# A hybrid short-convolution and gated linear-attention layer in streamed blocks: how keys and values are turned to token rows

## The chip, the cores and the metric

The kernel runs on one core of a Trainium2 chip. The metric is the device time of one execution in microseconds (us); lower is better. Before the change three executions took 2580.45, 2583.85 and 2586.18 us. The profile that is read below is of a further execution, which took 2583.43 us.

The engines are named as the profile names them: PE is the matrix engine (PEld its weight loads), DVE is VectorE, ACT is ScalarE, POOL is GpSimd, SP is the engine whose queue issues most loads. A trailing q (SPq, POOLq) is the engine's instruction queue.

## What is computed

One layer, float32, over 2048 prompt tokens and 64 sample tokens, width 1024. A wide input projection gives ten parts; four of them feed a three-tap convolution path (path A), four feed a gated linear attention with eight heads of width 128 (path B), two are gates. Both paths are projected, gated, summed and projected again; a normalised, gated residual with a small per-layer embedding follows. What matters here is path B, per head and chunk of 64 tokens:

```python
def hgrn2_block(S, q, k, v, logf):
    b = jnp.cumsum(logf, axis=1)
    ref = b[:, (L - 1) // 2][:, None]
    qe = q * jnp.exp(b - ref)
    ke = k * jnp.exp(ref - b)
    att = jnp.where(causal, jnp.einsum('bthk,bshk->bhts', qe, ke), 0.0)
    o = jnp.einsum('bhts,bshv->bthv', att, v) + jnp.einsum('bthk,bhkv->bthv', q * jnp.exp(b), S)
    S_new = jnp.exp(b_last)[..., None] * S + jnp.einsum('bshk,bshv->bhkv', k * jnp.exp(b_last[:, None] - b), v)
    return S_new, o
```

The last product sums over tokens s. A matmul of PE sums over the 128 partitions, so for it both k and v must lie with tokens on the partitions. The projection leaves them the other way round, with features on the partitions and tokens along the row.

## The kernel before

The 2112 tokens are worked off in three blocks of 768, 704 and 640 (`SIZES`, line 30). Within a block the order is: path B for the eight heads (`path_b`), with the gate projections (`gates`) run between heads as fill; path A (`path_a`); the output projections; the norms. Large projections run by a seven-product scheme: `sgroup` does two columns of weights in seven products of 12 matmuls, and after each product it calls `hook()`, which takes the next small step from a list. The attention of a head is cut into such steps (`head_attn`, a generator with a `yield` after each), and `path_b` writes out by hand which step runs after which product. `placed()` ties a step's matmuls behind the last matmul of the projection, so PE's order is the written one. On the other engines the framework orders the instructions by their dependencies and their place in the program; `tc.issue_after` and `behind_all` add an order on one engine.

`head_prep` makes what a head needs. It runs a projection group for f and v (`sgroup` with `sink_f`), takes the logarithm (line 959), the running sum (line 962), runs the next group for q and the output gate, and in its middle (`scaled`, called at the third product) makes the scaled keys `ka` and `kb`. `queries` then makes `qe` (line 1011 in the first block, 1015 and 1016 in the others) and `qx`, which is `qe` times the chunk factors `f` (line 1017). Chunks go in pairs of 128 tokens: six pairs in the first block, five in each of the others, which the parts of the block take as four and the rest. The middle block also has the 64 sample tokens, which make a part of their own (`single`).

Keys and values come to token rows in two ways.

- In the first block (`first`), and for the sample part: PE transposes each pair of `kb` and of `vt` (lines 1091 and 1093) into PSUM, and ACT copies both out (lines 1095 and 1096).
- In the other two blocks: `turned` lets DVE turn 32 x 32 squares (line 1051) into a scratch tile (`qx` for the values, `b` for the keys, which are free at that time), and POOL's queue writes the result to DRAM (line 1053). `in_rows` reads it back through POOL's queue with the squares moved to their places (line 1058). The values come back with each pair in four runs of 32 elements. The keys come back interleaved: the elements of one pair lie `npair` = 5 elements apart, and `kt[:, i]` takes every fifth. Both reads stand behind both writes and behind the last `pow` on POOL (`behind_all([*wrote, *powers])`).

Then, per part, `head_attn` makes the scores (lines 1106 and 1107), masks them, multiplies keys by values (line 1121, with `kt` as the weights and `v` as the moving operand), updates the states on DVE (line 1138), makes the outputs (line 1161 with `v` moving, line 1163 with `qx` as weights), norms them (POOL has the `pow` in `rstd_of`, line 689), transposes back (line 1179) and multiplies by the gate (line 1181).

Tiles `r` come from one pool of 48 (`RING`), whatever they hold.

Of the kernel before, what the change touches and what calls it, by code (L numbers as in the profile page):

```python
# [14 lines left out]
ALU = mybir.AluOpType  # L15
# [3 lines left out]
P = 128  # L19
# [4 lines left out]
CH = 64  # L24
# [69 lines left out]
def hybrid_step(  # L94
# [17 lines left out]
    V, A, G, T, SP = nc.vector, nc.scalar, nc.gpsimd, nc.tensor, nc.sync  # L112
# [13 lines left out]
    def nm(s):  # L126
        uid[0] += 1
        return f"{s}_{uid[0]}"
# [12 lines left out]
    def sized(bl, steps):  # L141

        while True:
            with sized_to(bl):
                try:
                    made = next(steps)
                except StopIteration:
                    return
            yield made

    def hn():
        return width[0] // 2

    def rt(n=0, dt=F32):
        t = ring.tile([P, BN + 2], dt, tag="r", name=nm("r"))
        return t if n is None else t[:, : n or width[0]]

    def hf(n=0):
        return ring.tile([P, HN], F32, tag="hf", name=nm("hf"), bufs=HALVES)[:, : n or hn()]

    def ps_attn():
        return psa.tile([P, 512], F32, tag="pa", name=nm("pa"))
# [14 lines left out]
    ident = const.tile([P, P], F32, tag="ident", name="ident")  # L177
# [116 lines left out]
    last, hooks, copies, adds, ahead, evicted, freed, powers, means = [None], [], [None], [None], [], [], [], [], []  # L294

    def placed():

        return tc.issue_after(last[0]) if last[0] is not None else nullcontext()
# [7 lines left out]
    def behind_all(marks):  # L306

        order = ExitStack()
        for ins in marks:
            order.enter_context(tc.issue_after(ins))  # L310
        return order
# [383 lines left out]
    def spread(cols, n):  # L695

        pb = ps_attn()
        with placed():
            for i, o in tiles_of(n):
                T.transpose(pb[:, o : o + P], cols[:, i : i + 1].to_broadcast([P, P]), ident)  # L700
        return pb[:, :n]
# [38 lines left out]
    def row_rstd(bl, out):  # L740

        todo = tiles_of(bl["n"])
        full = bl["n"] // P
        cols = small.tile([P, 2, 6], F32, tag="rows", name=nm("rows"), bufs=1)[:, 0, : len(todo)]
        nxt = []
        for n in range(0, len(todo) + 2, 2):
            now, nxt = nxt, []
            for i, o in todo[n : n + 2]:
                xts = [rt(512), rt(512)]
                for q, xt in enumerate(xts):  # L750
                    G.dma_start(xt, x_tok[bl["t0"] + o : bl["t0"] + o + P, q * 512 : q * 512 + 512])
                nxt.append((i, xts))
            for i, xts in now:
                sc = small.tile([P, 2], F32, tag="ss2", name=nm("ss2"), bufs=2)
                with behind_all(copies):
                    for q, xt in enumerate(xts):
                        A.activation(xt, xt, AF.Square, accum_out=sc[:, q : q + 1])
                V.tensor_tensor(sc[:, 0:1], sc[:, 0:1], sc[:, 1:2], ALU.add)
                rstd_of(sc[:, 0:1], cols[:, i : i + 1], 1.0 / D)
            yield  # L760
        pt, t = ps_attn(), rt(P)
        with placed():
            T.transpose(pt[: len(todo), :P], cols, ident)
        A.copy(t[: len(todo)], pt[: len(todo), :P])
        row = dram.tile([BN], F32, tag="xrs", name=nm("xrs"), bufs=2)[: bl["n"]]
        G.dma_start(row[: full * P].rearrange("(i p) -> i p", p=P), t[:full])
        if full < len(todo):
            G.dma_start(row[full * P :].unsqueeze(0), t[full : full + 1, (full + 1) * P - bl["n"] :])
        out.append(row)
        yield  # L770
# [162 lines left out]
    def chunks(t):  # L933
        return t.rearrange("p (c t) -> p c t", t=CH)

    def head_prep(bl, hc, hd, first, hs):
        n, npair = bl["n"], bl["npair"]
        nch, np1 = n // CH, npair * P
        sf, vt = rt(), rt()
# [15 lines left out]
        else:  # L955
            sgroup(FF * 8 + hd, IV * 8 + hd, hc, sink_f, first)
        lg, b, eq, qx = rt(), rt(), rt(), rt()
        wrote = None if first else [turned("tv", vt, qx, npair)]
        A.activation(lg, sf, AF.Ln, bias=lb[:, hd : hd + 1], scale=omlb[:, hd : hd + 1])
        if not first:  # L960
            V.tensor_scalar(sf, sf, nomlb[:, hd : hd + 1], omlb[:, hd : hd + 1], ALU.mult, ALU.add)
# [4 lines left out]
        f, r = qc[:, 0, :nch], qc[:, 1, :nch]  # L966
        ka, kb, qe, z = hf(npair * CH), rt(), rt(), rt()

        def scaled(after):
# [31 lines left out]
            if not first:  # L1001
                wrote.append(turned("tk", kb, b, npair))
# [5 lines left out]
        def queries():  # L1008
            if first:
                A.activation(qe, qe, AF.Silu)  # L1010
                V.scalar_tensor_tensor(qe, qe, QK_SCALE, eq, ALU.mult, ALU.mult)
            else:
                sq = rt()
                A.activation(sq, qe, AF.Sigmoid)
                V.scalar_tensor_tensor(qe, qe, QK_SCALE, sq, ALU.mult, ALU.mult)
                V.tensor_tensor(qe, qe, eq, ALU.mult)
            V.tensor_tensor(chunks(qx), chunks(qe), f.unsqueeze(2).to_broadcast([P, nch, CH]), ALU.mult)

        def sink_q(c, h, x, y):
            if c == 1:  # L1020
# [9 lines left out]
            sgroup(ZB * 8 + hd, QQ * 8 + hd, hc, sink_q, first, mid=scaled, free=first)  # L1030
        with tc.issue_after(freed[0]) if first else nullcontext():
            queries()
        by_token = None
        if not first:
            with behind_all([*wrote, *powers]):
                by_token = [in_rows(kind, npair) for kind in ("tv", "tk")][::-1]
        return dict(
            eq=eq, f=f, ka=ka, kb=kb, qe=qe, qx=qx, vt=vt, z=z, by_token=by_token,
            more=npair - 2 * SWAP, first=first, last=bl["last"], carry=None,
# [2 lines left out]
    def cols3(t, nt):  # L1042
        return t[:, : nt * P].rearrange("p (g c) -> p g c", c=P)
# [3 lines left out]
    def turned(kind, src, out, npair):  # L1047

        n = npair * P
        blocks4 = out[:, :n].rearrange("p (j a g) -> p g j a" if kind == "tk" else "p (j g a) -> p g j a", j=4, a=32)  # L1050
        V.transpose(blocks4, src[:, :n].rearrange("p (g b j) -> p g j b", b=32, j=4))
        turning[kind] = dram.tile([P, n], F32, tag=f"{kind}{npair}", name=nm(kind), bufs=2)
        return G.dma_start(turning[kind], out[:, :n]).ins

    def in_rows(kind, npair):

        t = rt(npair * P)
        G.dma_start(t.rearrange("q (i c) -> q i c", i=4), turning[kind].rearrange("(i b) (j c) -> (b j) i c", i=4, j=4))
        return t.rearrange("q (k g) -> q g k", g=npair) if kind == "tk" else t.rearrange("q (i g a) -> q g i a", i=4, a=32)

    def head_attn(ip, gs, d, hd):

# [2 lines left out]
        nt, ln = len(gs), gs[0]["len"]  # L1065
        o0, n = gs[0]["off"], nt * ln
        qe, z, att = d["qe"], d["z"], atts[ip]
        single = ln < P
        assert (nt == 2 * SWAP) == (o0 == 0)
        rows = slice(P - ln, P)  # L1070

        def tile3(i=None):
            if single and i is not None:
                return lone[i]
            if nt == 1:
                return small.tile([P, 1, P], F32, tag="one", name=nm("one"), bufs=5)
            return cols3(rt(nt * P), nt)

        def cols(t, g):
            end = g["off"] + ln  # L1080
            return t[:, end - P : end]

        if d["by_token"] is not None and not single:
            kt, v = (t[:, o0 // P : o0 // P + nt] for t in d["by_token"])
        else:
            p_k, p_v = ps_attn(), ps_attn()
            with placed():
                for i, g in enumerate(gs):  # L1090
                    T.transpose(p_k[:, i * P : i * P + P], cols(d["kb"], g), ident)
                for i, g in enumerate(gs):
                    T.transpose(p_v[:, i * P : i * P + P], cols(d["vt"], g), ident)
            kt, v = tile3(0), tile3(1)
            A.copy(kt[rows], cols3(p_k, nt)[rows])
            A.copy(v[rows], cols3(p_v, nt)[rows])
        p_a = ps_attn()
        with placed():
            for i, g in enumerate(gs):
# [371 lines left out]
    with tc.high_priority():  # L1471
# [3 lines left out]
        rows, xs, w1 = [], [], {}  # L1475
# [58 lines left out]
    for n in range(4):  # L1534
# [5 lines left out]
        with behind_all(done):  # L1540
            for i in range(3 * n, 3 * n + 3):
                t, total = rows[i], ss[:, i % 2, i // 2 : i // 2 + 1]
# [20 lines left out]
    with behind_all(done):  # L1563
        rs = rt()
        cols = [spread(ss[:, 0, 3 * h : 3 * h + 3], hn()) for h in range(2)]
# [30 lines left out]
    for bi, bl in enumerate(blocks):  # L1596
        first, kept = bi == 0, kepts[bi]
# [7 lines left out]
        a = []  # L1605
        nxt = None if bl["last"] else blocks[bi + 1]
        cols, a_first = [], []
        rows = sized(nxt, row_rstd(nxt, cols)) if nxt else iter(())
# [133 lines left out]
```

## Time and profile before

| what | value |
|---|---|
| median of three executions | 2583.85 us |
| the profiled execution | 2583.43 us |
| its span, first to last instruction | 2581.7 us |
| DVE busy | 1770.1 us, 69% of the span |
| ACT busy | 1491.8 us, 58% |
| POOL busy | 407.0 us, 16% |

How to read it: the span is the part of an execution in which the core's instructions run; the 1.7 us beside it lie around it. Busy times are unions of an engine's instructions. Matmuls overlap in the profile (the next one starts before the end that is shown for the last), so a matmul's price on PE is the distance between the starts of successive matmuls and not the duration that a row gives. In rows of a timeline the columns are start, length, engine, line, operation, tiles (out<-in), shapes and count; in rows of one line they are the shortest, median and longest duration in ns, and the first and last start in us.

### The profile page before, as it was taken

How to read it: one execution, taken by the hardware profiler on the slowest of the kernel's cores; microseconds unless marked ns; L12 is line 12 of the kernel's file. 1: busy time of each engine (PE TensorE's matmuls, PEld its weight loads, DVE VectorE, ACT ScalarE, POOL GpSimd, SP SyncE). 2: the span in 40 equal slices, each digit the busy share in tenths (PEclk: the TensorE clock that was granted, in tenths of full speed). 3: DMA queues.
4: the chain of work that ended last, by engine and by line, in shares of the span. 5: the costliest groups of instructions: out<-in, count | busy, mean ns of one | idle time of the engine just before them, and what ended most of it. 6: DMA issues, size and time to landing. Idle time of an engine off the chain costs nothing.

```text
span 2581.7 us, 47221 instructions
## 1 busy us (share of the span) xinstructions
PE 2562.9 (99%) x16198; PEld 2548.5 (99%) x16198; DVE 1770.1 (69%) x3541; ACT 1491.8 (58%) x2896; POOL 407.0 (16%) x741
## 2 busy tenths in 40 slices
PE   9999999999999999999999999999999999999999
PEld 9999999999999999999999999999999999999998
DVE  7788788898867775476564556887346655336967
ACT  6666666554454763465554555567456665446675
POOL 2011111230022021122111221102111111001011
PEclk9999999999999999999999999999999999999999
DMA  8678777998797887978878998989888898999986
GB/s 328 226 263 303 257 269 264 329 370 295 256 340 255 274 315 264 308 261 272 302 261 288 343 395 312 323 284 338 298 299 285 289 311 277 300 299 320 339 273 201
DMA packets 366865, 760.83 MB, mean 295 GB/s; under 512 B 45142, under 2 KB 49808, under 8 KB 366624
## 3 DMA queue, kind: packets, MB, share of 16 engines
q1 hardware_dynamic: 321696, 582.69, 66.2%
q0 software_dynamic: 44928, 175.12, 18.9%
q8 instruction: 128, 2.10, 0.3%
q14 instruction: 113, 0.93, 0.1%
HBM read 553.92 MB, written 203.71 MB: 293 GB/s over the span
## 4 chain that ended last, share of the span: by engine, by line
PE 90%; issue 3%; DVE 3%; DMA 2%; ACT 1%; POOL 0%; SPq 0%; DVEq 0%; POOLq 0%; ACTq 0%
PE pg L442 19%; PE pg L444 19%; PE pg L443 19%; PE pg L594 4%; PE pg L593 4%; PE pg L595 4%; PE pg L633 3%; PE pg L632 3%; PE pg L631 3%; PE pa L1121 2%; PE pa L1161 1%; PE pa L1163 1%; PE pa L1107 1%; DMA raw<-w_blk 1%; PE pa L1106 1%
## 5 line engine op out<-in xcount | busy, mean ns | idle before, releaser
L442 PE MATMUL pg<-r,hi 128*128 128x320 f32 (+2 forms) x3304 | 1084.3, 328 | 0.0
L443 PE MATMUL pg<-r,hi 128*128 128x320 f32 (+2 forms) x3304 | 1067.9, 323 | 0.0
L444 PE MATMUL pg<-r,lo 128*128 128x384 f32 (+2 forms) x2356 | 768.4, 326 | 2.3 <-DMA lo<-low 2.3
L273 ACT CAST hi<-raw 128x512 fp32r<-128x512 f32 x730 | 449.9, 619 | 507.7 <-PE pg L443 188.1
L442 PEld LDWEIGHTS pg<-r,hi 128*128 128x128 f32 x3304 | 622.9, 189 | 0.9 <-issue 0.2
L443 PEld LDWEIGHTS pg<-r,hi 128*128 128x128 f32 x3304 | 622.3, 188 | 0.0
L444 PEld LDWEIGHTS pg<-r,lo 128*128 128x128 f32 x2356 | 442.9, 188 | 3.2 <-DMA lo<-low 3.2
L444 PE MATMUL pg<-r,s 128*128 128x352 f32 (+1 forms) x948 | 300.6, 317 | 1.7 <-DMA s<-low 1.7
L594 PE MATMUL pg<-r,hi 128*128 128x320 f32 (+2 forms) x864 | 277.4, 322 | 1.9 <-DVE r L226 1.9
L593 PE MATMUL pg<-r,hi 128*128 128x320 f32 (+2 forms) x864 | 274.9, 322 | 0.0
L226 ACT CAST hi<-raw 128x512 fp32r<-128x512 f32 x252 | 155.4, 621 | 167.4 <-PE pg L443 45.6
L226 DVE TENSOR_TENSOR r<-r,r 128x320 fp32r<-128x320 f32 (+7 forms) x354 | 208.9, 609 | 48.7 <-ACT r L226 47.5
L226 ACT CAST r<-r 128x320 fp32r<-128x320 f32 (+7 forms) x354 | 185.5, 557 | 42.7 <-DVE r L1293 8.2
L226 DVE TENSOR_TENSOR lo<-raw,hi 128x512 fp32r<-128x512 f32 x231 | 157.8, 687 | 76.1 <-ACT hi L226 72.5
L444 PEld LDWEIGHTS pg<-r,s 128*128 128x128 f32 x948 | 178.5, 188 | 2.5 <-DMA s<-low 2.4
L595 PE MATMUL pg<-r,lo 128*128 128x352 f32 (+2 forms) x564 | 180.8, 321 | 0.0
L226 ACT CAST hi<-s 128x512 fp32r<-128x512 f32 x156 | 96.6, 619 | 145.4 <-PE pg L443 121.4
L632 PE MATMUL pg<-r,hi 128*128 128x384 f32 (+2 forms) x512 | 167.2, 327 | 0.2 <-DVE r L226 0.2
L594 PEld LDWEIGHTS pg<-r,hi 128*128 128x128 f32 x864 | 162.2, 188 | 4.0 <-DVE r L226 3.6
L631 PE MATMUL pg<-r,hi 128*128 128x384 f32 (+2 forms) x512 | 165.8, 327 | 0.2 <-ACT hi L273 0.2
L456 ACT COPY hf<-pg 128x352 f32<-128x352 f32 (+2 forms) x354 | 157.2, 446 | 11.7 <-PE pg L444 10.7
L593 PEld LDWEIGHTS pg<-r,hi 128*128 128x128 f32 x864 | 161.3, 188 | 1.2 <-ACT r L226 0.6
(398 smaller groups left out, 4120.2 us busy)
## 6 DMA issues: line engine op xcount, KB each, us to landing
raw<-w_blk SPq DMA_DIRECT2D x577, 256.0 KB, 4.4
raw<-S SPq DMA_DIRECT2D x444, 256.0 KB, 4.5
lo<-low SPq DMA_DIRECT2D x422, 256.0 KB, 4.3
s<-low SPq DMA_DIRECT2D x308, 256.0 KB, 4.4
low<-lo SPq DMA_DIRECT2D x271, 256.0 KB, 3.8
S<-s SPq DMA_DIRECT2D x152, 256.0 KB, 3.6
low<-r POOLq DMA_DIRECT2D x54, 256.0 KB, 5.3
r<-w_blk POOLq DMA_DIRECT2D x52, 256.0 KB, 6.5
```

The lines of the kernel that those rows point to most:

```text
L226: return A.copy(hi, src).ins, V.tensor_tensor(lo, src, hi.bitcast(F32), ALU.subtract).ins
L273: A.copy(hi, raw)
L442: add(hi[:, k, :], xhi, start=start and k == 0, stop=False)
L443: add(hi[:, k, :], xlo, start=False, stop=False)
L444: last[0] = add(lo[:, k, :], xhi, start=False, stop=k == KH - 1).ins
L456: copied = A.copy(got[n], ps[bank])
L593: add(hi[:, k, :], xhi, start=start and k == 0, stop=False)
L594: add(hi[:, k, :], xlo, start=False, stop=False)
L595: last[0] = add(lo[:, k, :], xhi, start=False, stop=k == KH - 1).ins
L631: T.matmul(ps, hi[:, k % 4, :], xhi[:, c], start=k == ks[0], stop=False)
L632: T.matmul(ps, hi[:, k % 4, :], xlo[:, c], start=False, stop=False)
L633: last[0] = T.matmul(ps, lo[:, k % 4, :], xhi[:, c], start=False, stop=k == ks[-1]).ins
```

## The change

Four edits, all in path B.

1. `turned` writes the keys' squares in the order that the values have. `in_rows` reads them back in that order, and POOL then copies them into a further tile so that each pair lies in 128 elements side by side. `kt[:, i]` so becomes a row of adjacent elements.
2. In the first block the values, too, are turned by DVE and go through DRAM; its keys are still transposed by PE and copied by ACT.
3. In the first block `qx` is made by POOL, not by DVE.
4. `head_attn` takes from PE what did not come by DRAM: nothing in the later blocks' pairs, the keys in the first block, both for the sample part. Transposes and copies of one operand now stand together.

```diff
-        wrote = None if first else [turned("tv", vt, qx, npair)]
+        wrote = [turned("tv", vt, qx, npair)]
...
-            V.tensor_tensor(chunks(qx), chunks(qe), f.unsqueeze(2).to_broadcast([P, nch, CH]), ALU.mult)
+            (G if first else V).tensor_tensor(chunks(qx), chunks(qe), f.unsqueeze(2).to_broadcast([P, nch, CH]), ALU.mult)
...
-        by_token = None
-        if not first:
-            with behind_all([*wrote, *powers]):
-                by_token = [in_rows(kind, npair) for kind in ("tv", "tk")][::-1]
+        with behind_all([*wrote, *powers]):
+            by_token = [in_rows(kind, npair) for kind in (("tv",) if first else ("tv", "tk"))][::-1]
...
-        blocks4 = out[:, :n].rearrange("p (j a g) -> p g j a" if kind == "tk" else "p (j g a) -> p g j a", j=4, a=32)
+        blocks4 = out[:, :n].rearrange("p (j g a) -> p g j a", j=4, a=32)
...
-        return t.rearrange("q (k g) -> q g k", g=npair) if kind == "tk" else t.rearrange("q (i g a) -> q g i a", i=4, a=32)
+        t = t.rearrange("q (i g a) -> q g i a", i=4, a=32)
+        if kind == "tv":
+            return t
+        kt = rt(npair * P)
+        G.tensor_copy(kt.rearrange("q (g i a) -> q g i a", i=4, a=32), t)
+        return cols3(kt, npair)
...
-        if d["by_token"] is not None and not single:
-            kt, v = (t[:, o0 // P : o0 // P + nt] for t in d["by_token"])
-        else:
-            p_k, p_v = ps_attn(), ps_attn()
+        ready = [] if single else [t[:, o0 // P : o0 // P + nt] for t in d["by_token"]]
+        for q, src in enumerate((d["kb"], d["vt"])[: 2 - len(ready)]):
+            turn_ = ps_attn()
             with placed():
                 for i, g in enumerate(gs):
-                    T.transpose(p_k[:, i * P : i * P + P], cols(d["kb"], g), ident)
-                for i, g in enumerate(gs):
-                    T.transpose(p_v[:, i * P : i * P + P], cols(d["vt"], g), ident)
-            kt, v = tile3(0), tile3(1)
-            A.copy(kt[rows], cols3(p_k, nt)[rows])
-            A.copy(v[rows], cols3(p_v, nt)[rows])
+                    T.transpose(turn_[:, i * P : i * P + P], cols(src, g), ident)
+            ready.insert(q, tile3(q))
+            A.copy(ready[q][rows], cols3(turn_, nt)[rows])
+        kt, v = ready
```

## The prediction, made before the changed kernel ran

> **What bounds the kernel.** The first page gives the engines' shares and the chain of work that ended last.
>
> ```profile
> span 2581.7 us, 47221 instructions
> PE 2562.9 (99%) x16198; PEld 2548.5 (99%) x16198; DVE 1770.1 (69%) x3541; ACT 1491.8 (58%) x2896; POOL 407.0 (16%) x741
> PE 90%; issue 3%; DVE 3%; DMA 2%; ACT 1%; POOL 0%; SPq 0%; DVEq 0%; POOLq 0%; ACTq 0%
> ```
>
> Busy shares alone would not prove that PE is the bound, since matmuls overlap. So the waits come next, those of PE alone, longest total first (total us, times, longest).
>
> ```profile
> PE pa L700 <- POOL cols L689: 3.4, 6, 0.8
> PE pg L444 <- DMA lo<-low: 2.3, 1, 2.3
> ```
>
> The two largest totals are 3.4 and 2.3 us in 2582: PE is fed nearly all the time. A matmul pass that goes away, or is issued closer to the one before, shortens the kernel by as much, unless PE then waits for something new. All the other engines matter only as suppliers.
>
> **The key-value product.** Its line is read for each block by itself, in the order of the blocks.
>
> ```profile
> L1121 PEld LDWEIGHTS pa<-r,r x96: 187/192/192, 103.4 to 471.6; 128*128 128x128 f32 x96
> ...
> L1121 PEld LDWEIGHTS pa<-r,r x80: 297/316/319, 1097.0 to 1360.8; 128*128 128x128 f32 x80
> ...
> L1121 PEld LDWEIGHTS pa<-r,r x80: 302/314/321, 1926.7 to 2161.2; 128*128 128x128 f32 x80
> ```
>
> The same 128x128 weight load takes 192 ns in the first block, where the keys lie side by side, and some 315 ns in the other two, where they lie five elements apart. (There are two passes for each pair: 8 heads x 6 pairs x 2 = 96, and 8 x 5 x 2 = 80.) What this costs PE is read from starts in the timeline, one part of four pairs in the first block and one whole head in the second.
>
> ```profile
> 103.38 0.34 PE L444 MATMUL pg<-r,lo 128*128 128x384 f32 x1
> 103.56 1.05 PE L1121 MATMUL pa<-r,r 128*128 128x128 f32 x8
> 104.36 0.42 PE L442 MATMUL pg<-r,hi 128*128 128x384 f32 x1
> ...
> 1096.95 0.33 PE L444 MATMUL pg<-r,lo 128*128 128x352 f32 x1
> 1097.12 2.33 PE L1121 MATMUL pa<-r,r 128*128 128x128 f32 x10
> 1099.20 0.41 PE L442 MATMUL pg<-r,hi 128*128 128x352 f32 x1
> ```
>
> From the projection's matmul before to the one after: 0.98 us for eight side-by-side passes, 2.25 us for ten interleaved ones. Two more side-by-side passes would cost 0.22 us at the 0.11 us of a transpose (next fence), so ten would take 1.20 us. **Saved: 1.05 us a head, 16 heads, 16.8 us.**
>
> **The values' transposes in the first block.**
>
> ```profile
> 95.80 0.60 PE L1091 MATMUL pa<-ident,r 128*128 128x128 f32 x4
> 96.23 0.60 PE L1093 MATMUL pa<-ident,r 128*128 128x128 f32 x4
> 96.67 0.39 PE L1106 MATMUL pa<-r,hf 128*128 128x128 f32 x2
> ...
> L1093 PE MATMUL pa<-ident,r x48: 272/272/273, 96.2 to 463.2; 128*128 128x128 f32 x48
> ```
>
> Four value transposes hold PE for 0.44 us, 0.11 each. All 48 of the first block go: **5.3 us saved.** The 16 copies by ACT that go with them are off the path, and their going is counted as nothing. Together 22.1 us.
>
> **The key copy on POOL.** This is the one new link on a short chain: the DRAM read lands, POOL copies 128x640, PE loads the weights. Before, PE read the landed tile directly. Here are the reads of the keys that open the second and the third block and that of the third block's last head, each with its time to landing, then the product of that last head; the third block's first product starts at 1926.7 by the third row of the second fence above, the second block's at 1097.0.
>
> ```profile
> 1085.90 0.76 POOL L1058 DMA_DIRECT2D r<-tk  x1 [3.67 <-DMA tk<-r]
> ...
> DMA to landing us min/median/max: 6.9/6.9/6.9
> ...
> 1918.61 0.76 POOL L1058 DMA_DIRECT2D r<-tk  x1 [4.23 <-PE pg L444]
> ...
> DMA to landing us min/median/max: 6.7/6.7/6.7
> ...
> 2151.69 0.76 POOL L1058 DMA_DIRECT2D r<-tk  x1 [4.17 <-issue]
> 2152.44 0.19 POOL L889 COPY r<-hist_p 128x2 f32<-128x2 f32 x1
> ...
> DMA to landing us min/median/max: 6.8/6.8/6.8
> ...
> 2159.36 2.35 PE L1121 MATMUL pa<-r,r 128*128 128x128 f32 x10
> ```
>
> The slack, from landing to weight load, is 1097.0 - 1092.8 = 4.2 us in the second block's first head; worked out in the same way for each head, that block never has less than 4.0. In the third block it is 1926.7 - 1925.3 = 1.4 in the first head and, the load being 0.15 before the product at 2159.36, 2159.2 - 2158.5 = 0.7 in the last; the six between are 2.3, 2.5, 1.0, 2.6, 13.9 and 2.8. What must fit into it is the copy and POOL's reaction to a landing. For the reaction there is a row: the keys' write before the last read, and its landing.
>
> ```profile
> 2144.99 0.60 POOL L1053 DMA_DIRECT2D tk<-r  x1 [6.08 <-DVE r L1051]
> ...
> DMA to landing us min/median/max: 6.2/6.2/6.2
> ```
>
> It landed at 2151.2, and the read that waited for it began at 2151.69: 0.5 us. DVE gives back about 0.1: the turns of line 1051 (row below) go from 1.32 to 1.46 us, the values' at the short end and the keys' at the long one, and the keys get the values' form. So 0.4 plus the copy.
>
> The copy itself is nowhere in this trace. The nearest rows on POOL:
>
> ```profile
> 62.26 0.20 POOL L202 MEMSET r<- 128x128 f32 x1
> 62.53 0.48 POOL L203 TENSOR_SCALAR_AFFINE_SELECT r<-r 128x128 f32<-128x128 f32 x1
> ...
> 60.63 1.69 POOL L203 TENSOR_SCALAR_AFFINE_SELECT r<-r 128x128 f32<-128x128 f32 x2
> ...
> L916 POOL COPY hist_p<-r 128x2 f32<-128x2 f32 x24 | 6.5, 269 | 343.6 <-DVE r L896 343.6
> ```
>
> A copy of two elements takes 0.27 us and a fill of 128 takes 0.20, so the fixed part is some 0.2 us. A select over 128 elements, which reads and writes like a copy and computes besides, takes 0.48 us in one case and 1.69 for the two others, 0.85 each: 2.2 to 5 ns an element above the fixed part. Carried to 640 elements: 1.6 to 3.2 us. From below, the fill may be all fixed part, and then the copy is hardly over 0.3. A copy is the simplest of these, so I take the faster select: **1.6 us**. Then 2.0 us must fit. PE waits 0.6 + 1.0 + 1.3 = **2.9 us** in three heads of the third block, nothing in the second. At 0.3 us nothing waits; at 3.2 us (3.6 to fit) it is 2.2 + 1.3 + 1.1 + 2.6 + 1.0 + 0.8 + 2.9 = 11.9 us.
>
> [...]
>
> Behind the waiting copy on POOL: in the last head the short copy of line 889 (start 2152.44, above) would stand up to 8 us later if it is queued behind; its reader on ACT comes a projection group later. One such place in each of two blocks, taken as nothing; without that cover it costs a microsecond.
>
> **The first block's new work.** DVE gets a turn and loses a product in each head.
>
> ```profile
> 60.00:460.00 400.00, 400.00 (x2476) 399.00 (x2475) 327.84 (x648) 262.83 (x510) 53.36 (x92) 1.00 0.76 266
> ...
> L1051 DVE STREAM_TRANSPOSE r<-r x32: 1319/1380/1464, 1066.6 to 2143.3; 128x640 f32<-128x640 f32 x32
> ...
> L1017 DVE TENSOR_TENSOR r<-r,qc 128x768 f32<-128x768 f32 x8 | 7.6, 951 | 0.0
> ...
> 112.78 1.76 DVE L962 TENSOR_TENSOR_SCAN r<-keep,r 128x768 f32<-128x768 f32 x1 [1.41 <-ACT r L959]
> ```
>
> In 400 us of the first block DVE (the third engine, 327.84 us) is busy 82%. The turn of 768 elements is 1.32 x 768/640 = 1.6 us, against 0.95 that goes: +0.65 us a head, 5.2 in all. The turn falls just ahead of the running sum, where DVE idles 1.41 us for ACT's logarithm; what is not covered there costs DVE some 0.2 us, and PE nothing, as DVE is idle for a sixth of the stretch. Without this cover a late weight split would cost PE up to 1.6 us a head, 12.8 us.
>
> The values must be back before line 1121, and `qx` before line 1163. The second head, whose sum is the row above:
>
> ```profile
> 134.82 0.95 DVE L1017 TENSOR_TENSOR r<-r,qc 128x768 f32<-128x768 f32 x1
> ...
> 155.72 1.05 PE L1121 MATMUL pa<-r,r 128*128 128x128 f32 x8
> ...
> 163.79 0.39 PE L1163 MATMUL pa<-r,r 128*128 128x128 f32 x2
> ```
>
> The values are turned by about 113. A write and a read of some 7 us each end near 127, 28 us before 155.72. Even a read that POOL issues only behind its own product, at about 137, would land by 145. `qx` has 29 us; were POOL four times as slow as DVE, 4 us, it would be hidden. Only the first head is short: its product by keys is at 103.56, its `qx` at about 96.5, so a read behind that product would cost it once some 4 us. Value: nothing. The 16 transfers of 384 KB add 6 MB to 761; PE's waits for DMA, above, are so few that I count nothing.
>
> **Sum**, against the profiled execution's 2583.4 us: - 16.8 - 5.3 + 2.9 = 2564.2 us. The median of the runs is 0.4 above that execution, so 2564.5. With the copy's bounds the sum runs from 2561.7 to 2573.6.
>
> **The rivals.**
>
> *The copy is slow.* At the slower select's rate PE waits 11.9 us: 2573.6. For it speak two of three selects; against it, that a copy computes nothing. 13 in 100.
>
> *The copy eats the gain (slower).* Place: the wait of line 1121 in the third block, then in the second as well. With seven heads whose slack sums to 13.3 us the loss is 7 x (copy + 0.4) - 13.3, and beyond 4.0 us to fit the second block adds its own. It equals 22.1 us at a copy of 4.4 us; from there the kernel is slower. At 6 us the third block loses 31.5 and the second 10.1: 2603. For it: POOL's instructions are uneven (0.48 and 0.85 us for one select). Against: it takes twice the slower select's rate. 9 in 100. [...]
>
> *DVE is too full in the first block.* Each turn delays a weight split: up to 12.8 us lost, 2577. Against it stands the idle sixth. 7 in 100.
>
> *The spacing of the keys isn't what slows line 1121.* The values' four runs of 32 differ between the blocks, too. Then only the 5.3 us are saved, less up to 2.9 for the copy: 2578.5 to 2581.4, no change. Against it: it is the weight load, of keys, that grew from 192 to 315 ns. 5 in 100.
>
> **How the numbers follow.** The forecast has 66 in 100. About 0.2%, 5 us, is what a measurement of this kernel can tell from no change, so faster means below 2578.7: the forecast, the slow copy and most of the full DVE, 84 in 100. Within 0.2%: the spacing and the rest of DVE, 7. Slower: 9. The range runs from 2557 (the sum with a copy that is wholly hidden, less the runs' own scatter of some 4) to 2576 (the slow copy, with 2.5 on top).
>
> **What would show it.** Right: line 1121's weight loads at 190 ns in all blocks, ten passes in 1.2 us; line 1093 without the first block's 48; PE's waits with a new entry, line 1121 for POOL, of about 3 us, all in the third block; POOL copies of 128x640 of about 1.6 us. Wrong: a copy over 3 us, PE waiting for it in the second block, PE waiting for DVE's weight splits between 60 and 460 us, or weight loads still at 300 ns.

## The result, and the profile after

| | before | after |
|---|---|---|
| median of six executions each, in turn on one chip | 2582.76 us | 2561.78 us |
| lowest to highest | 2580.45 to 2586.18 | 2558.75 to 2564.96 |
| the profiled execution | 2583.43 | 2561.54 |

After against before is 0.9918, with a 95% interval of 0.9905 to 0.993: 21.0 us, or 0.8%, faster. The forecast was 2564.5 us.

The head of the page of the changed kernel:

```profile
span 2559.8 us, 47168 instructions
...
PE 2540.1 (99%) x16150; PEld 2525.1 (99%) x16150; DVE 1778.2 (69%) x3541; ACT 1485.7 (58%) x2880; POOL 451.0 (18%) x781
```

PE has 48 matmuls fewer and 22.8 us less to do, ACT 16 instructions fewer. POOL has 44 us more. PE stays the bound: it is busy for 99% of the span, and the largest totals of its waits are 4.1 and 3.2 us. These waits (total us, times, longest), the longest two and those of line 1106:

```profile
PE pg L444 <- DMA lo<-low: 4.1, 3, 2.3
PE pa L700 <- POOL cols L689: 3.2, 6, 0.8
...
PE pa L1106 <- ACT r L1095: 1.0, 1, 1.0
PE pa L1106 <- DVE r L1016: 0.8, 1, 0.8
```

The entry that the prediction looked for, line 1121 waiting for POOL, is not in the list at all. One small entry is new: line 1106 once waits 1.0 us for ACT's copy of line 1095. Next, the product's weight loads block by block (shortest, median and longest ns, first and last start) and its ten passes in the timeline:

```profile
L1121 PEld LDWEIGHTS pa<-r,r x96: 187/192/193, 102.5 to 467.5; 128*128 128x128 f32 x96
...
L1121 PEld LDWEIGHTS pa<-r,r x80: 187/192/192, 1095.2 to 1348.5; 128*128 128x128 f32 x80
...
L1121 PEld LDWEIGHTS pa<-r,r x80: 188/192/192, 1913.8 to 2139.6; 128*128 128x128 f32 x80
```

```profile
1095.20 0.32 PE L444 MATMUL pg<-r,lo 128*128 128x352 f32 x1
1095.37 1.28 PE L1121 MATMUL pa<-r,r 128*128 128x128 f32 x10
1096.40 0.40 PE L442 MATMUL pg<-r,hi 128*128 128x352 f32 x1
```

All three blocks now load weights in 192 ns, and ten passes take 1096.40 - 1095.20 = 1.20 us, the size that was forecast. The two new tasks of POOL, then the third block's last head on POOL, where the slack was smallest in the profile before, and that read's own time to landing:

```profile
L1061 POOL COPY r<-r 128x640 f32<-128x640 f32 x16 | 11.5, 716 | 94.1 <-DMA r<-tk 82.1 <-PE pg L443 12.0
...
L1017 POOL TENSOR_TENSOR r<-r,qc 128x768 f32<-128x768 f32 x8 | 19.9, 2488 | 21.5 <-DVE r L1011 21.3
```

```profile
2124.26 0.60 POOL L1051 DMA_DIRECT2D tk<-r  x1 [5.96 <-DVE r L1049]
...
2129.44 0.76 POOL L1056 DMA_DIRECT2D r<-tk  x1 [1.61 <-issue]
2135.91 0.72 POOL L1061 COPY r<-r 128x640 f32<-128x640 f32 x1 [5.72 <-DMA r<-tk]
```

```profile
DMA to landing us min/median/max: 6.4/6.4/6.4
```

The read lands at 2129.44 + 6.4 = 2135.84 and the copy begins 0.07 us later; it ends at 2136.63, and the product that needs it starts at 2138.72, some 2 us on. The copy takes 0.72 us and not 1.6.

The first block's stretch, in the columns of the prediction's row (PE, PEld, DVE, ACT, POOL busy; clock; DMA share; GB/s):

```profile
60.00:460.00 400.00, 399.00 (x2457) 397.73 (x2456) 340.10 (x654) 259.28 (x499) 84.00 (x117) 1.00 0.83 284
```

DVE was busy 327.84 us there and now is 340.10, though it lost a product in every head. That is more than the +5.2 us of the prediction. Part of it is no added work: six more instructions (x648, now x654) fall into the same 400 us, since PE is some 4 us ahead by their end. Experiment 3 finds the rest.

### The profile page after: what moved, and what is told of

The parts are those of the page before. It is cut to its first block, busy times and chain, and to the rows that moved or that the text cites. A ratio compares the mean times of both kernels' runs of the same rounds, so it can differ in the third digit from the quotient of the medians.

```text
span 2559.8 us, 47168 instructions
## 1 busy us (share of the span) xinstructions
PE 2540.1 (99%) x16150; PEld 2525.1 (99%) x16150; DVE 1778.2 (69%) x3541; ACT 1485.7 (58%) x2880; POOL 451.0 (18%) x781
## 3 DMA queue, kind: packets, MB, share of 16 engines
q0 software_dynamic: 46464, 181.41, 19.8%
## 4 chain that ended last, share of the span: by engine, by line
PE 76%; issue 3%; DVE 3%; DMA 3%; ACT 1%; POOL 0%; SPq 0%; DVEq 0%; ACTq 0%; POOLq 0%
PE pg L442 16%; PE pg L444 16%; PE pg L443 16%; PE pg L594 4%; PE pg L593 4%; PE pg L595 4%; PE pg L633 3%; PE pg L632 3%; PE pg L631 3%; DMA lo<-low 1%; DMA raw<-w_blk 1%; PE pa L1121 1%; PE pa L1161 1%; PE pa L1163 1%; PE pa L1107 1%
```

## The experiments

Each kernel ran with runs of the kernel before on the same chip, which had medians of 2582.68, 2581.91 and 2582.22 us in the three sets.

### 1. The keys alone, and the change again beside them

Edit 1 on the kernel before; everything in the first block as before.

```diff
-        blocks4 = out[:, :n].rearrange("p (j a g) -> p g j a" if kind == "tk" else "p (j g a) -> p g j a", j=4, a=32)
+        blocks4 = out[:, :n].rearrange("p (j g a) -> p g j a", j=4, a=32)
...
-        return t.rearrange("q (k g) -> q g k", g=npair) if kind == "tk" else t.rearrange("q (i g a) -> q g i a", i=4, a=32)
+        t = t.rearrange("q (i g a) -> q g i a", i=4, a=32)
+        if kind == "tv":
+            return t
+        kt = rt(npair * P)
+        G.tensor_copy(kt.rearrange("q (g i a) -> q g i a", i=4, a=32), t)
+        return cols3(kt, npair)
```

> The kernel before with the first edit alone: keys turned in the values' order and copied side by side by GpSimd; the first block is as before. Theory: the key-value product gains 1.05 us a head in 16 heads and the copy is hidden, so 16.8 us less than before, 2566 us beside a before of 2583. Rival (spacing of the keys is not the cause): within 3 us of before, with the weight loads of line 1121's product still at 315 ns. Rival (the copy costs): less than 14 us gained, and TensorE waits for GpSimd at that product.

> The keys-only kernel once more, as the partner of the changed kernel in this call: 2565 to 2567 us; the theory's difference to the changed kernel is 4 us, the rival's below 1.5.

> The changed kernel once more, in the same call as the keys-only kernel. Two readings differ so far: beside the keys-only kernel the first block's edits look worth 5 us (2561.8 against 2566.7, in different calls), beside the kernel before they look worth nothing (the values-only kernel at 2582.5 against 2582.7). Theory (48 transposes at 0.11 us, less a wait for ScalarE of about 1 us): 4 us less than the keys-only kernel of this call. Rival (the first block's edits give back what they save): within 1.5 us of it.

| kernel | median us (runs) | ratio to before, 95% interval |
|---|---|---|
| keys alone | 2566.68 (5) | 0.9937, 0.9925 to 0.9949 |
| keys alone, third set | 2563.31 (5) | 0.9921, 0.9904 to 0.9939 |
| the whole change, third set | 2561.35 (6) | 0.9915, 0.9896 to 0.9933 |

The keys alone bring 16.0 and 18.9 us, against 16.8 forecast for the passes. The whole change is 2.0 us better than the keys alone in the set that they share, between the 4 us of the one theory and the 1.5 us of the other, and the runs' ranges overlap (2557.3 to 2565.2 against 2559.5 to 2565.1). So this set does not decide how much of the 5.3 us of the first block arrives.

### 2. The first block alone

The changed kernel with the old key path in `turned` and `in_rows`: the reverse of the diff above.

> The changed kernel without the first edit: keys interleaved as before, without a copy; the first block's values by VectorE and DRAM, its queries' product on GpSimd. Theory: only the 48 transposes go, 5.3 us, less what the new wait of the scores for ScalarE in the first block takes (1.2 us in the changed kernel's profile): 4 to 5 us less than before. Rival (VectorE too full in the first block): no gain, TensorE waiting for VectorE's weight splits between 60 and 460 us.

> The values-only kernel once more, for a second profile. Its first 700 us hold the same instructions in the same order on each engine as the changed kernel's, yet its profile had TensorE wait 3.1 us for VectorE's weight splits between 528 and 560 us (VectorE waiting for stores to land), which the changed kernel's did not. Theory (scatter of the transfers between executions): other waits this time, the stretch from the first block's last key-value product to the second block's first one below 632 us, against 634.8. Rival (something fixed, such as where the tiles lie in memory): the same waits at 528 to 560 us, and 634 to 636 us again.

Twelve runs have a median of 2582.53 us, ratio 0.9996 (0.9986 to 1.0005): no gain that can be told, where 4 to 5 us were expected. A single further run took 2580.56. In this kernel the product's weights are loaded in 316 ns again in the later blocks, so the 192 ns belong to edit 1 alone.

Where did the 48 transposes go? From the first head's key-value product to the eighth's, in the first block, this kernel takes 365.1 us (weight loads from 103.2 to 468.3), the changed one 365.0 (102.5 to 467.5), where before had 368.2 (103.4 to 471.6). Seven heads hold 42 of the transposes, 4.6 us at 0.11; 3.1 to 3.2 us arrive. Most of the rest is the new wait of the changed kernel:

```profile
356.18 0.43 PE L1106 MATMUL pa<-r,hf 128*128 128x64 f32 x2 [1.00 <-ACT r L1095]
```

PE gets to the second part's scores earlier than before and finds ACT still copying the first part's keys out of PSUM. The wait is there in the changed kernel and in this one, in both executions of each, and in experiments 3, 4 and 5, which have the same edits; it is not in the kernels with keys alone. In the single further run it is the shortest, 0.5 us, and there the distance is 364.5 us, so that 3.7 us arrive.

The remainder is lost later, and not alike from run to run. Here are the kernel of this experiment and the changed kernel between the first block's heads and the second's, a stretch in which both issue the same instructions in the same order; first the windows, then the two longest waits of the kernel of this experiment in it.

```profile
470.00:1090.00 620.00, 612.86 (x3553) 609.45 (x3552) 457.41 (x772) 319.57 (x612) 111.31 (x203) 0.99 0.86 296
```

```profile
470.00:1090.00 620.00, 615.32 (x3581) 612.05 (x3580) 458.32 (x775) 321.06 (x614) 112.53 (x203) 1.00 0.87 298
```

```profile
PE pg L444 <- DMA lo<-low: 3.5, 2, 2.9
PE pg L444 <- DVE lo L226: 2.9, 4, 1.2
```

The second execution has 28 matmuls more in the same 620 us, at a granted clock a little higher. PE waits 7.0 us in this stretch here; in before's profile it is 3.3, in the changed kernel's 4.2 and 3.3 (two executions), in that of the single further run 5.2. That run passed from the first block's last product to the second block's first 3.6 us faster (467.1 to 1095.0, here 468.3 to 1099.8), so at least that part of the loss is scatter. It is as large as the whole gain of the first block: by trace the first block's edits are worth 3 to 4 us where they act, by medians between 0.2 (this experiment) and 2.0 to 4.9 (whole change against keys alone, within a set and across sets).

The runs sorted by their mean granted clock say more. At a clock of 1.000 the kernel of this experiment took 2574.36 and 2576.07 us, and before, in the same set, 2579.04 to 2580.97 (five runs). At that clock the whole change took 2557.32 to 2558.79 (three of its twelve runs over the sets), the keys alone 2559.45 to 2566.68 (seven of ten). In the mean that is 4.5 and 5.2 us for the first block's edits, near the 5.3 of the forecast; at 0.999 it is 1.1 and 3.7. The runs are few, and in the two windows above PE's waits and the clock differ together (7.0 us at 0.99, 4.2 at 1.00), so this does not say what lowered the clock. It does say where the gain can be had: in executions that keep the clock.

### 3. The product `qx` back on VectorE

```diff
-            (G if first else V).tensor_tensor(chunks(qx), chunks(qe), f.unsqueeze(2).to_broadcast([P, nch, CH]), ALU.mult)
+            V.tensor_tensor(chunks(qx), chunks(qe), f.unsqueeze(2).to_broadcast([P, nch, CH]), ALU.mult)
```

> The changed kernel with the first block's queries multiplied by the chunk factors on VectorE again. Theory: the product is hidden on either engine, since VectorE idles a sixth of that stretch: within 2 us of the changed kernel. Rival (the move to GpSimd is what makes room for the turn on VectorE): 2 to 13 us slower than the changed kernel, with TensorE waiting for VectorE in the first block.

2563.82 us (6 runs), ratio 0.9937 (0.9924 to 0.995); the changed kernel had 2561.78 in another set. Moving the product to POOL has therefore no effect on the time that can be told. The window of the first block in this kernel:

```profile
60.00:460.00 400.00, 399.21 (x2456) 397.96 (x2455) 340.30 (x661) 259.09 (x498) 64.60 (x110) 1.00 0.82 285
```

DVE is busy 340.30 us with the products and 340.10 without: taking eight products of 0.95 us away, 7.6 us, gave DVE 0.2 (0.45 in the changed kernel's second execution, 339.85). The changed kernel's timeline shows where the time is lost: a product of POOL, what VectorE does beside it, and a product beside which VectorE is idle.

```profile
236.66 2.92 POOL L1017 TENSOR_TENSOR r<-r,qc 128x768 f32<-128x768 f32 x1 [0.71 <-DVE r L1011]
...
237.56 0.68 DVE L352 TENSOR_TENSOR s<-s,raw 128x512 f32<-128x512 f32 x1
238.17 0.54 DVE L462 TENSOR_TENSOR hf<-hf,pg 128x384 f32<-128x384 f32 x1
238.63 1.50 DVE L226 TENSOR_TENSOR lo<-raw,hi 128x512 fp32r<-128x512 f32 x1
...
339.46 1.47 POOL L1017 TENSOR_TENSOR r<-r,qc 128x768 f32<-128x768 f32 x1 [2.74 <-DVE r L1011]
```

The longest of the groups concerned (count | busy us, mean ns of one | idle before), in the kernel with the product on VectorE and in the changed kernel:

```profile
L226 DVE TENSOR_TENSOR lo<-raw,hi 128x512 fp32r<-128x512 f32 x71 | 48.6, 686 | 6.2 <-ACT hi L226 6.2
```

```profile
L226 DVE TENSOR_TENSOR lo<-raw,hi 128x512 fp32r<-128x512 f32 x71 | 51.0, 719 | 8.3 <-ACT hi L226 8.3
```

VectorE's first operations beside the product keep their time (0.68 and 0.54 us in the rows above, against means of 0.69 and 0.55 with the product on VectorE). The last one takes 1.50 us in place of 0.69 and ends 0.55 us behind the end that is shown for the product. So it is at seven of the eight products: one operation on two SBUF tiles lasts 0.8 to 1.3 us longer, 6.6 us in all. At the eighth VectorE is idle, and the product takes 1.47 us; beside a working VectorE it takes 1.84 to 3.06. All seven have two SBUF inputs, but others with two, such as the one at 237.56 with 0.68 us, kept their time, so no run shows what decides which operation is slowed. The price here was 6.6 us for the 7.6 that were moved off.

### 4. The copy five times

```diff
-        G.tensor_copy(kt.rearrange("q (g i a) -> q g i a", i=4, a=32), t)
+        for _ in range(5):
+            G.tensor_copy(kt.rearrange("q (g i a) -> q g i a", i=4, a=32), t)
```

> The changed kernel with GpSimd's copy of the keys made five times over, one after the other. Theory (the copy is free only because it fits between the landing and the product): five copies of 0.716 us and a reaction of 0.1 make 3.7 us. In the changed kernel's trace the product starts 1.65, 1.3, 2.6, 2.6, 2.2, 14.8, 2.7 and 2.7 us after the landing in the third block's eight heads, and never less than 4.5 us after it in the second block. So TensorE should wait 2.0, 2.4, 1.1, 1.1, 1.5, 0, 1.0 and 1.0 us there, 10 us in all, and nothing in the second block: 2572 us, up to 4 us more where the granted clock drops to half for 3.4 us behind a long wait. Rival (the order on TensorE or GpSimd gives way, or the trace's slack is not the real one): within 3 us of the changed kernel, or over 20 us slower with waits in the second block, too.

The profiled execution took 2575.04 us, the median of ten runs is 2585.37, ratio 1.001 (0.9999 to 1.0021): the whole gain is gone. Waits of PE and the copies' row in that profile:

```profile
PE pa L1122 <- POOL r L1062: 9.9, 7, 2.4
```

```profile
L1062 POOL COPY r<-r x80: 712/721/1022, 1089.7 to 2150.8; 128x640 f32<-128x640 f32 x80
```

With 5 x 0.72 = 3.6 us of copies, seven of the third block's eight products wait, 9.9 us in all, where 10 were expected. That is near what the rival *the copy is slow* had for a copy of 3.2 us and 0.4 beside it (11.9 us). The profiled execution's loss against the changed kernel, 13.5 us, is more than the waits, and the median is 13 us above the 2572 that were expected. Three of the waits in the timeline, and the windows behind the second:

```profile
1916.09 1.38 PE L1122 MATMUL pa<-r,r 128*128 128x128 f32 x10 [2.41 <-POOL r L1062]
...
1948.81 2.41 PE L1122 MATMUL pa<-r,r 128*128 128x128 f32 x10 [2.09 <-POOL r L1062]
...
1981.91 1.38 PE L1122 MATMUL pa<-r,r 128*128 128x128 f32 x10 [0.90 <-POOL r L1062]
```

```profile
1948.80:1952.40 3.60, 3.59 (x16) 3.59 (x17) 1.57 (x3) 1.17 (x2) 0.00 (x0) 0.53 0.30 112
1953.00:1956.00 3.00, 3.00 (x24) 3.00 (x23) 2.86 (x6) 1.77 (x4) 0.83 (x2) 1.00 0.70 208
```

For some 3.4 us behind the wait at 1948.8 the granted clock is half, and the ten passes take 2.41 us in place of the others' 1.38; then it is full again. The longer wait at 1916.1 has no such loss behind it. The mean granted clock of a run goes with that: 0.999 in the two shortest runs (2575.0 and 2577.5 us), 0.996 or 0.997 in the eight others. By estimate, at 0.9965 an execution of 2585 us has lost 0.0035 x 2585 = 9.0 us to it, at 0.999 2.6 us; the difference, 6 us, is some two thirds of the 10 us between the short runs and the long. The wait of 2.09 us so cost, by estimate, 2.09 + 3.4 / 2 = 3.8 us.

### 5. The distance between the keys

Every pair copied by itself, into a tile in which the elements of a row lie two, three or four apart; all else as in the changed kernel, except that five small copies a head take the place of one. The number is `s`.

```diff
+        out = []
...
+            kt = rt(m * P * s)
+            for e in range(m):
+                one = kt[:, e * P * s : (e + 1) * P * s].rearrange("q (k s) -> q k s", s=s)[:, :, 0]
+                G.tensor_copy(one.rearrange("q (i a) -> q i a", a=32), t[:, g0 + e])
+                out.append(one)
+        return out
```

> The changed kernel with the keys copied so that a pair's elements lie two apart (8 bytes) instead of side by side; ten small copies a head do it where one did. Only the weight loads of the key-value product are of interest here. [...] Rival (any spacing costs): about 315 ns, as with five apart.

> The same with three elements between (12 bytes). [...] Rival (proportion to the spacing): about 235 ns.

> The changed kernel with the keys of a pair four elements apart (16 bytes). Two apart took 194 ns a weight load. [...] Rival (the time grows in proportion to the spacing): 260 to 290 ns.

The product's weight loads in the second and third block, two apart, then three, then four:

```profile
L1127 PEld LDWEIGHTS pa<-r,r x160: 193/196/197, 1092.0 to 2139.1; 128*128 128x128 f32 x160
```

```profile
L1127 PEld LDWEIGHTS pa<-r,r x160: 251/261/263, 1091.9 to 2146.6; 128*128 128x128 f32 x160
```

```profile
L1127 PEld LDWEIGHTS pa<-r,r x160: 307/330/332, 1094.6 to 2158.1; 128*128 128x128 f32 x160
```

| elements apart | weight load, ns | one execution, us |
|---|---|---|
| 1 (the changed kernel) | 192 | 2561.54 |
| 2 | 196 | 2561.93 |
| 3 | 261 | 2569.78 |
| 4 | 330 | 2580.64 |
| 5 (before) | 315 | 2583.43, without the first block's edits |

The distance sets the load, and the time follows it; in none of the three does PE wait for POOL at this product. Two apart is nearly as good as side by side, and four apart is no better than five. The rival that the time grows in proportion to the distance falls: it had about 235 ns for three apart and 260 to 290 for four. So does the one that any spacing costs: it had about 315 ns for two apart. Why the load of 196 ns at two apart grows to 261 at three and 330 at four, no run shows.

### 6. The first block's keys by the same way

Seven of the first block's eight heads get their keys, too, by DVE, DRAM and POOL's copy; this takes 42 more transposes from PE.

```diff
-            if not first:
+            if not first or hd > 0:
...
-            by_token = [in_rows(kind, npair) for kind in (("tv",) if first else ("tv", "tk"))][::-1]
+            by_token = [in_rows(kind, npair) for kind in (("tv",) if first and hd == 0 else ("tv", "tk"))][::-1]
```

> The changed kernel, and in heads 1 to 7 of the first block the keys go by VectorE, DRAM and the GpSimd copy too; head 0 keeps the transposes. Theory: 42 more transposes of 0.11 us leave TensorE, 4.6 us, and the wait of the scores for ScalarE goes with them: 4.6 to 6 us less than the changed kernel, 2556 us. The keys are ready some 20 us ahead of the scores' successor, so the path of about 16 us is covered. Rival (VectorE too full: one more turn of 1.6 us a head at 82 to 84 percent busy): TensorE waits for weight splits in the first block, and the time is no better than the changed kernel's or worse by up to 11 us.

2587.02 us (11 runs), ratio 1.0018 (1.001 to 1.0027), where 2556 was expected. PE's longest waits, then POOL and ACT in the timeline of the stretch that the second of them belongs to, and its windows:

```profile
PE pg L442 <- ACT r L853: 9.1, 3, 7.7
PE pg L442 <- DVE r L490: 8.3, 1, 8.3
PE pg L442 <- ACT hi L226: 3.5, 1, 3.5
```

```profile
247.52 1.07 POOL L1061 COPY r<-r 128x768 f32<-128x768 f32 x1 [3.62 <-DMA r<-tk]
248.54 1.12 POOL L379 DMA_DIRECT2D r<-w_blk  x2
...
257.46 0.62 ACT L226 CAST r<-r 128x512 fp32r<-128x512 f32 x1 [11.74 <-DMA r<-w_blk]
```

```profile
255.00:259.00 4.00, 0.00 (x0) 0.00 (x0) 0.89 (x2) 1.54 (x3) 0.00 (x0) 1.00 0.17 61
259.30:266.10 6.80, 3.08 (x10) 3.11 (x11) 6.80 (x15) 4.01 (x8) 1.96 (x4) 0.50 0.83 271
```

POOL waits 3.62 us for the keys' landing, and the issues of the next weights (line 379) stand behind its copy. ACT has to split one of these weights next and idles 11.74 us for it; VectorE waits for ACT, and PE for VectorE: 4 us of the first window without one matmul, and the 6.8 us behind it at half the clock. In the changed kernel the longest wait of ACT for weights of line 379 in this block is 3.1 us. The three waits, 20.9 us, and the clock (0.995 as a mean over the runs, against 0.999 before: by estimate 0.004 x 2587 = 10 us) come to about 31 us, the distance between 2556 and 2587; the sum is rough, as it puts one execution's waits beside the mean clock of all.

So the copy was taken off POOL in the first block: ACT makes it, after the second part's scores, and no copy on POOL's queue holds back issues there.

```diff
-        if kind == "tv":
+        if kind == "tv" or npair == blocks[0]["npair"]:
...
+        late = d["first"] and len(d["by_token"]) == 2
+        if late and ip == 0:
+            d["runs"] = d["by_token"][0]
+            d["side"] = rt(blocks[0]["npair"] * P)
+            d["by_token"] = [cols3(d["side"], blocks[0]["npair"]), d["by_token"][1]]
...
+        if late and ip == 1:
+            with behind_all(copies):
+                A.copy(d["side"].rearrange("q (g i a) -> q g i a", i=4, a=32), d["runs"])
```

> As the kernel with the first block's keys by DRAM in heads 1 to 7, but there ScalarE copies the keys side by side, behind the scores of the second part, some 5 us ahead of the product; GpSimd's queue gets no copy in the first block. Theory (that kernel lost because GpSimd's copy waited 3 to 4 us for its landing with the loads for the weight sums queued behind it, and ScalarE, VectorE and TensorE then waited for these): without the copy in that queue the waits of 8.5, 7.9 and 3.7 us of TensorE in the first block are gone, and the 42 transposes less show: 2557 to 2560 us. Rival (VectorE is too full with one more turn of 1.6 us a head): several waits of TensorE for VectorE in the first block remain, and the time is 2565 us or more.

2570.52 us (7 runs), ratio 0.9958 (0.9943 to 0.9973): 16.5 us better than the kernel with POOL's copy, so most of that loss went with the copy; still some 9 us behind the change as it is. PE's waits in the first block, the longest wait of ACT behind two of them, and the window of the block:

```profile
PE pa L1187 <- DVE r L1182: 1.9, 4, 0.9
PE pg L442 <- ACT hi L226: 1.4, 1, 1.4
PE pg L444 <- DVE lo L226: 0.9, 1, 0.9
PE pa L1129 <- ACT r L1123: 0.7, 1, 0.7
```

```profile
349.79 0.62 ACT L226 CAST r<-r 128x512 fp32r<-128x512 f32 x1 [7.57 <-DMA r<-w_blk]
```

```profile
60.00:460.00 400.00, 395.01 (x2401) 390.79 (x2400) 345.88 (x650) 250.43 (x486) 86.32 (x129) 1.00 0.83 293
```

PE waits 4.9 us in this block, against 1.0 in the changed kernel. Two causes stand side by side. VectorE is busy 345.88 us of 400 with a second turn in each head, and four waits, 1.9 us, are for its line 1182: that is the way of the prediction's rival of a full DVE. But the waits of 1.4 and 0.9 us, at 351.0 and 352.5, come right behind ACT's 7.57 us without weights. The issues of line 379 still come late, at 339.6 to 344.2 us where the changed kernel has them at 325.8 and 335.1: they stand behind the keys' write and read on POOL's queue, and that write waited 9.6 us for VectorE's turn. ACT's waits for these weights come to 3.1 us in this block of the changed kernel, 21.6 with POOL's copy and 13.0 here. The busy share alone tells nothing: it is 86% here and 85% in the changed kernel. Which of the two causes weighs more was not tried. Of the versions tried, the change itself is the fastest.

## Why the prediction was right

**The bound and the key-value product.** Right, in kind and in size: 16.8 us forecast, 16.0 and 18.9 measured with the keys alone. Experiment 5 shows that the distance between elements is the cause, so the rival that the spacing isn't what slows line 1121 falls. The profiled pair gives some 3 us more in the later blocks, and part of that is a clock: before waited 1.43 us at 1123.5 (line 1106, for line 1016) and ran at half clock behind it; the changed kernel waits 0.81 us there and keeps the full clock. Before's wait and the window behind it:

```profile
1123.53 0.46 PE L1106 MATMUL pa<-r,hf 128*128 128x128 f32 x2 [1.43 <-DVE r L1016]
```

```profile
1125.30:1128.60 3.30, 3.30 (x14) 3.30 (x13) 0.71 (x3) 0.40 (x1) 0.00 (x0) 0.50 1.04 366
```

3.4 us at half clock are, by estimate, 1.7 us lost. This belongs to one execution: in its second one the changed kernel waits 1.91 us at the same place and has the half clock behind it. No step of the prediction had it.

**The copy on POOL.** The term that was mis-sized: 2.9 us of waits forecast, none measured. Both of its parts were too long. The copy was carried over from the faster select at 1.6 us and is 0.72. The reaction was read as 0.5 us from a DMA issue that followed a landing; the copy, already waiting at the head of its queue, starts 0.07 us after it. Some 0.8 us must fit instead of 2.0. The slack itself was no constant: the last head had 0.7 us before, and now some 2 remained even behind the copy, since its read was issued 5.2 us after the keys' write (2124.26 to 2129.44) and not 6.7 (2144.99 to 2151.69). Experiment 4 confirms the mechanism that the term rested on: with 3.6 us of copies the third block waits in seven heads and the second in none. It corrects its price, too: the prediction counted waits at their length, and behind some of them the clock halves (behind that of 2.09 us in experiment 4), so a slow copy would have cost more than the 11.9 us given to it. The prediction had the whole gain gone at a copy of 4.4 us; in the median 3.6 us of copies were enough.

**The first block's transposes.** The 48 passes left, yet the 5.3 us were not wholly had: 3.1 to 3.2 of 4.6 us in seven heads, with a wait for line 1095 in place of most of the rest. The prediction counted the going of ACT's copies as nothing and did not ask what PE, arriving earlier, finds not ready. How much survives to the end varied from run to run: 4.5 and 5.2 us among executions at full clock, less by the medians (experiment 2).

**The first block on DVE and POOL.** PE has no wait for DVE there, as forecast, but by another account. DVE's added work was taken as turns less products, 5.2 us; its busy time in the window grew by 12.3. Some 3 of these are the six instructions more, and the rest is above 5.2 since beside POOL's products VectorE lost nearly what the move relieved (6.6 of 7.6 us). These parts are durations, which overlap at their ends (by 0.07 us in the rows of experiment 3, 237.56 + 0.68 against 238.17), so they don't add up to the busy time. The cover (idle DVE) was wide enough. The rival of a full DVE did not take place in this kernel.

**The sum.** 2564.2 us forecast for the profiled execution, 2561.5 measured. That the two are so close is in part luck: a miss of 3.5 us stands against two of about 3 us the other way. The wait of 2.9 us did not come. By the second block's first product the changed kernel was ahead by 1.8 us (1097.0 against 1095.2) and not by 5.3. From there to the third block's last product it gained 19.8 us more (2161.2 against 2139.6 at the end), not 16.8; by estimate 1.7 of these 3 us are the clock, and the rest was not traced.

## What to carry to other kernels

Lay the weights of small matmuls close: with 4-byte elements up to 8 bytes apart a load took 192 to 196 ns here, from 12 bytes on 261 to 330. The row to look for is one line's weight loads with different durations in different stages. Moving an elementwise product with SBUF operands to GpSimd relieved VectorE by 0.2 us of 7.6, so such a move is to be booked at nothing until VectorE's own rows beside it are read. And a copy that waited 3.62 us for a landing on POOL's queue held back the issues of line 379 behind it, and ACT then waited 11.74 us for weights and PE 8.29 us for VectorE (experiment 6): put such a copy on an engine that issues no loads (ACT here, 16.5 us better), or where the landing is certain to be past.

## What the runs showed of the hardware

- POOL's copies of 128x640 take 716 ns. Those of 128x128 in experiment 5 take 305 (the group below), so by estimate an element costs (716 - 305) / 512 = 0.80 ns and the start 0.20 us.

```profile
L1066 POOL COPY r<-r 128x128 f32<-128x128 f32 x80 | 20.7, 305 | 96.2 <-DMA r<-tk 66.4 <-PE pg L443 24.1 <-PE pa L1099 5.7
```

- A weight load with elements three apart (261 ns) lies between two (196) and four (330) apart; five apart (315) is no worse than four.
- Half the clock for some 3.4 us came behind waits of 1.43 and 2.31 us (before, at 1123.5 and 934.0), of 2.32 us (the changed kernel, at 931.6) and of 2.09 us (experiment 4, at 1948.8). It came neither behind one of 0.90 us (experiment 4, at 1981.9, where the ten passes took 1.38 us in all) nor behind longer ones of 2.41 us (experiment 4, at 1916.1) and 2.71 us (the changed kernel's second execution, at 930.9), so the length of a wait alone does not decide. What decides which wait is followed by it was not tried.
